# A GLA and RWKV-7 decoder layer on one core: one bit-trick step less in the inverse square root, the gate's scale folded into other factors, and pairs of half-width steps joined into one

## The chip, the core and the metric

The kernel runs on one core of one Trainium2 chip. A core has a matrix engine (TensorE, shown as PE for its matmuls and PEld for its weight loads), a vector engine (VectorE, DVE), a scalar engine (ScalarE, ACT), a general engine (GpSimd, POOL) and a queue that issues transfers (SyncE, SP). Each engine works through its own list of instructions in order, and semaphores make one engine wait for another. The metric is the device time of one launch in microseconds (us); lower is better.

## The reference, cut to what matters

One decoder layer over 4096 positions and 1024 channels. One input projection feeds two groups of heads: four heads of gated linear attention (GLA) and eight heads of RWKV-7. Both are gated with SiLU, joined and projected out. The parts that the change touches are these lines of RWKV-7 (per head of width 64):

```python
kk = kk / jnp.maximum(jnp.linalg.norm(kk, axis=-1, keepdims=True), 1e-12)
y = _rwkv7_scan(r_h, decay, k_h, v_h, kk, a)     # S_t = S_{t-1}(diag(w) - kk^T(a kk)) + v^T k
y = ((y - mu) * lax.rsqrt(var + RWKV_GN_EPS)).reshape(B, T, RWKV_W)
y = y * rwkv_ln_w + rwkv_ln_b
bonus = jnp.sum(r_h * k_h * rwkv_r_k, axis=-1, keepdims=True) * v_h
rwkv_out = (y + bonus) * jax.nn.silu(rg)
```

The norms of the layer (input, GLA heads, RWKV heads, the key norm `kk`, output) each need an inverse square root.

## The kernel before, in words

The sequence is cut into 8 blocks of 512 positions. In each block, the RWKV side has 4 units (pairs of heads; 128 partitions hold both heads, 64 each), so 32 units in all, and the GLA side has 2 pairs of heads. A unit's 512 positions are 8 chunks of 64. Projections are done in fp16 with the weights and the inputs split in a high and a low part (three products each, 24 matmuls of 128x512 per projection); the recurrences are in fp32.

The work of one RWKV unit, in the functions that the change touches:

- `newton` (lines 620 to 634) makes an inverse square root on DVE from sums of squares that a matmul with ones has left in PSUM: nine steps on tiles of 128x128. The first writes the value `nv`; the second shifts its bits right by one into `nt`; the third makes the first guess `ny` from `nt`; two rounds of three steps each refine it. It is called with three sets of tiles: `nya` (the key norm, 32 calls), `nyc` (the heads' norm after the recurrence, 32) and `nyg` (GLA heads, block input and block output, 32).
- `rwkv_ab` (780) makes a unit's operands: `rk`, `rn`, `E`, `kf`, `r`, `v`, `bk`, `De`, `Do`, the matrix `Nb`, the gate `rgs` and the bonus. The bonus is a row sum (`brow`, copied by ACT out of PSUM), written to memory, read back broadcast as `bv` (two transfers on SP's queue), and multiplied by `v`.
- `rwkv_i` (911) completes a 64x64 triangular inverse for each of 8 chunks and 2 heads from its two 32x32 diagonal blocks: DVE transposes one block (`Ta`), 16 matmuls make a product in rows 32 to 63 and 96 to 127 of a bank (`bank<-Ta,Nb`), DVE copies it (`Vs`, two copies of 32x256), 16 more matmuls (`bank<-Nb,Vs`) and two copies by ACT put the result in `Nb`.
- `rwkv_c` (935) runs the recurrence, 8 chunks in a chain. In each chunk PE makes `ch<-sv,De` and `ch<-sv,Do` for the two heads, ACT copies `us`, PE makes `ch<-us,Nb`, ACT makes two copies into `sv`, PE makes `ch<-sv,bk`, and DVE writes the next state `sv` with one SCALAR_TENSOR_TENSOR per head, which adds `psd`, the old state times the decay `PC`. ACT makes `psd` beside the chain, one step of 64x64 per head.
- `rwkv_d` (977) takes the recurrence's output `cy` and its square `crs`, takes the norm by `newton`, and then has four steps of 128x512 on DVE: `cy` times the norm; times `ln_w`, plus `bv`; plus `ln_b`, times the scale of the gate (`hinv`, half the inverse of the gate weights' scale); times the gate `rgs`, into `mgr`.

The order of the work isn't written by hand. The program first runs as eight generators (`stream_x` and its neighbours, 1306 to 1380) that take turns by priority. Each operation is recorded as a step with an estimated duration from `cost` (312). Then a list scheduler (`forward` and `backward`, 234 and 284) lays all steps out once forward, once back from the end and once forward again, and the instructions are issued, engine by engine, in the order of those estimated starts. So a changed cost or a removed step can move every later instruction on every engine, while what each instruction waits for stays bound to its data. A line of a helper that calls each recorded operation (368) is what the profile shows for nearly all instructions; they are told apart by their tiles.

PSUM has six shared banks for projections and small products, one bank for the recurrence's products (`ch`) and one for its output (`y`).

Of the kernel before, what the change touches and what calls it, by code (L numbers as in the profile page):

```python
# [20 lines left out]
P = 128  # L21
# [29 lines left out]
W_R, W_RK, W_RV, W_RG = 1, 5, 9, 13  # L51
# [9 lines left out]
PK_LW = 33  # L61
PK_LB = 37
# [18 lines left out]
def hymba_kernel(ctx, tc, xT, wt, wg, wo, wua, gup, pk, ck, out):  # L81
# [5 lines left out]
    one = ctx.enter_context(tc.tile_pool(name="one", bufs=1))  # L87
# [7 lines left out]

    TABLES = ("pkt", "scl", "invs", "hinv", "mu_s", "omu_s", "carry", "wosc", "woinv", "gnh")
    now = [0.0]
    streams = []  # L100
    ready, used, busy = {}, {}, {}
# [210 lines left out]
    def cost(eng, op, ins, n, o):  # L312

        big = [a for a in ins if math.prod(a.shape[1:]) > 1 or n == 1]
        few = len(ins) - len(big)
        psum = any(a.space == PSUM for a in ins)
        if eng == "V":
            fast = len(big) == 1 and not psum and op in ("tensor_scalar", "tensor_copy", "tensor_scalar_mul", "tensor_scalar_max")
            if op == "tensor_tensor_scan":
                return 0.068 + n / 480  # L320
            runs = 0.09 if n == 64 or len(o.shape) > 2 and o.shape[-1] == 64 and n == 512 else 0.0
            return 0.068 + 0.06 * (few > 0) + n / (1920 if fast else 960) + runs
        if eng == "G":
            return 0.225 + 0.07 * few + n * (2.13 if len(big) > 1 else 0.95) / 960
        return (0.1 if n == 64 and o.shape[0] == 64 else 0.0) + (0.052 if psum else 0.094) + n / 1200 + 0.09 * (few > 0)
# [143 lines left out]
    carry = sb(one, [P, 13], F32, "carry")  # L469
    V.memset(carry, 0.0)  # L470
    gnh = sb(one, [P, 4], F32, "gnh")


    Sst = [sb(one, [P, 64], F32, f"Sst{p}") for p in range(4)]
# [80 lines left out]
    def split_w(n, i):  # L555
        raw, hl = raws[n % 4], hls[n % 2]
        junk = hl.rearrange("p a k t -> p (a k t)").bitcast(F32).rearrange("p (k t) -> p k t", k=KT)
        iv = invs[:, i:i + 1]
        yield from absmax_scale(raw, scl[:, i:i + 1], iv, "W", junk)
        w = [hl[:, 0], hl[:, 1]]  # L560
        if n < ND:

            st = "r" if i < W_Q else "g"
            k = made[st]
            made[st] += 1
            if got[st] < k + (st == "g"):
                yield lambda: got[st] >= k + (st == "g")
            w = first[i] = pair(st)
        split(raw, scl[:, i:i + 1], *w)
        V.tensor_scalar(iv, iv, nwx[:, 9:10], 0.125 if W_Q <= i < W_K else 1.0, ALU.mult, ALU.mult)  # L570
        if W_R <= i < W_RG or i == W_WA:
            j = i - 1 if i else 12
            V.tensor_tensor(mu_s[:, j:j + 1], pkt[:, j:j + 1], iv, ALU.mult)
            V.tensor_tensor(omu_s[:, j:j + 1], omu[:, j:j + 1], iv, ALU.mult)
        elif i >= W_GG or W_RG <= i < W_Q:
            V.tensor_scalar_mul(hinv[:, i:i + 1], iv, 0.5)
            if i >= W_GG:
                h = i - W_GG
                V.tensor_tensor(gnh[:, h:h + 1], hinv[:, i:i + 1], pkt[:, PK_GN:PK_GN + 1], ALU.mult)
        if n < ND:  # L580
            for a in range(2):
                D.dma_start(wdr[i][a], w[a])
            split_done.add(i)
            done["W"] += 1
        else:
            store_w(i, hl)
# [33 lines left out]
    def newton(src, mul, add, mx, st):  # L620

        v = sb(rt, [P, P], F32, "nv" + NEWTON[st])
        y = sb(rt, [P, P], F32, "ny" + st)
        t = sb(rt, [P, P], F32, "nt" + NEWTON[st])
        if mx is not None:
            V.tensor_scalar_max(v, src, mx)
        else:
            V.tensor_scalar(v, src, mul, add, ALU.mult, ALU.add)
        V.tensor_scalar(t.bitcast(I32), v.bitcast(I32), 1, None, ALU.logical_shift_right)
        V.tensor_scalar(y.bitcast(I32), t.bitcast(I32), -1.0, float(0x5F1FFFF9), ALU.mult, ALU.add)  # L630
        for a, c in ((-0.703952253, 1.681913948), (-0.5, 1.5000003)):
            V.tensor_tensor(t, y, y, ALU.mult)
            V.scalar_tensor_tensor(t, t, a, v, ALU.mult, ALU.mult)
            V.scalar_tensor_tensor(y, t, c, y, ALU.add, ALU.mult)
        return y
# [144 lines left out]
    def rwkv_ab(u, p, b, xs, LR):  # L780
# [102 lines left out]
        pst = yield from need("r")  # L883
        stat_mm(pst, bones, r)
        brow = sb(rt, [P, P], F32, "brow", 1)
        S.copy(brow, pst[:, 0:P])
        bv = tA("bv", 2)
        bcast(brow, 2, bv, "b")
        V.tensor_tensor(bv, bv, v, ALU.mult)
# [21 lines left out]
    def rwkv_i(nb):  # L911

        Ta = sb(rt, [P, NC, 32], F32, "Ta", 1)
        Vs = sb(rt, [P, NC, 32], F32, "Vs", 1)
        yield after(nb)
        for q0 in (0, 64):
            V.transpose(Ta[q0:q0 + 32], nb[q0:q0 + 32, :, q0:q0 + 32])
        yield after(Ta)
        pl = (yield from need("i")).rearrange("p (a c t) -> p a c t", a=2, c=NC)
        for c in range(NC):  # L920
            for q0 in (0, 64):
                T.matmul(pl[q0 + 32:q0 + 64, 0, c, :], lhsT=nb[q0:q0 + 32, c, q0 + 32:q0 + 64], rhs=Ta[q0:q0 + 32, c, :],
                         start=True, stop=True)
        for q0 in (0, 64):
            V.tensor_copy(Vs[q0 + 32:q0 + 64], pl[q0 + 32:q0 + 64, 0])
        yield after(Vs)
        for c in range(NC):
            for q0 in (0, 64):
                T.matmul(pl[q0:q0 + 32, 1, c, :], lhsT=Vs[q0 + 32:q0 + 64, c, :], rhs=nb[q0 + 32:q0 + 64, c, q0 + 32:q0 + 64],
                         start=True, stop=True)  # L930
        for q0 in (0, 64):
            S.copy(nb[q0:q0 + 32, :, q0 + 32:q0 + 64], pl[q0:q0 + 32, 1])
        rel("i")

    def rwkv_c(p, b, mgt, st_):
        de, do, nb, sv, bkt, PC, bv, tg = st_
        yield after(nb, bkt, sv, ("y", 1))

        py = pbank("y").rearrange("p (c t) -> p c t", c=NC)
        st = Sst[p]  # L940
        S.copy(sv[0:64, 0, 0, :], st[0:64])
        V.tensor_copy(sv[64:128, 0, 1, :], st[64:128])
        dd = ((lo, de, 0), (hi, do, 1))
        for c in range(NC):
            pc = pbank("ch").rearrange("p (a t) -> p a t", a=8)
            for q_, d_, e in dd:
                T.matmul(pc[q_, 0, :], lhsT=d_[:, c, 0:64], rhs=sv[:, c, e, :], start=True, stop=True)
            us = sb(rt, [P, 64], F32, "us", 2)
            S.copy(us, pc[:, 0, :])
            for q_, d_, e in dd:  # L950
                T.matmul(py[q_, c, :], lhsT=sv[:, c, e, :], rhs=d_[:, c, 64:128], start=c == 0, stop=False)
            psd = sb(rt, [P, 64], F32, "psd", 2)
            for q_, d_, e in dd:
                S.activation(psd[q_], sv[q_, c, e, :], AF.Copy, scale=PC[q_, c])
            yield after(us) + XL
            T.matmul(pc[:, 1, :], lhsT=nb[:, c, 0:P], rhs=us, start=True, stop=True)
            S.copy(sv[lo, c, 0, :], pc[lo, 1, :])
            S.copy(sv[hi, c, 1, :], pc[hi, 1, :])
            yield after(sv) + XL
            T.matmul(pc[:, 2:4, :], lhsT=bkt[:, c, :], rhs=sv[:, c], start=True, stop=True)  # L960
            for q_, d_, e in dd:
                dst = sv[q_, c + 1, e, :] if c < NC - 1 else st[q_]
                V.scalar_tensor_tensor(dst, pc[q_, 2 + e, :], PC[q_, c], psd[q_], ALU.mult, ALU.add)
            if c < NC - 1:
                yield after(sv, ("ch", 1)) + XL
        for c in range(NC):
            for q_, d_, e in dd:
                T.matmul(py[q_, c, :], lhsT=sv[q_, c, e, :], rhs=nb[q_, c, P:192], start=False, stop=c == NC - 1)
        yield lambda: done["C"] == done["CC"]
        y = sb(rt, [P, TB], F32, "cy")  # L970
        rs = sb(rt, [P, TB], F32, "crs")
        S.copy(y, py.rearrange("p c t -> p (c t)"))
        S.activation(rs, y, AF.Square)
        done["CC"] += 1
        spawn(rwkv_d(p, b, mgt, y, rs, bv, tg), 2.5)

    def rwkv_d(p, b, mgt, y, rs, bv, tg):
# [11 lines left out]
            bcast(st, 2, rs, "c")  # L989
        V.tensor_tensor(y, y, rs, ALU.mult)  # L990
        rel("d")
        V.scalar_tensor_tensor(y, y, pkt[:, PK_LW + p:PK_LW + p + 1], bv, ALU.mult, ALU.add)
        i = W_RG + p
        V.tensor_scalar(y, y, pkt[:, PK_LB + p:PK_LB + p + 1], hinv[:, i:i + 1], ALU.add, ALU.mult)
        yield lambda: len(mfree["r"]) > 0
        mgt[4 + p] = mfree["r"].pop(0)
        V.tensor_tensor(mgt[4 + p], y, tg, ALU.mult)
        absmax(mgt, 4 + p, y)
        done["C"] += 1

# [453 lines left out]
```

## Time and profile before

| What | Before |
|---|---|
| median of 3 runs | 2419.3 us (2418.5 to 2422.08) |
| time of the profiled execution | 2425.58 us |
| its span, from the first instruction to the last | 2423.8 us |
| granted TensorE clock, mean | 0.982 |
| PE busy | 2301.9 us, 20710 matmul records |
| DVE busy | 1691.6 us |
| ACT busy | 1219.0 us |
| POOL busy | 851.4 us |

The profile comes from one execution, 1.8 us of which lie outside its span. A PE that is busy isn't always at its peak, since the ends of matmuls are modelled. In the groups of instructions, a row reads: line, engine, operation, tile written <- tiles read, shape, count, then busy time in us and the mean of one in ns, then the engine's idle time just before them and what ended it. An fp32 matmul has two records, one for each of its passes.

### The profile page before, as it was taken

The numbers are of one execution on the slowest core, as the hardware profiler recorded it, in microseconds if no ns is written. First come the engines' busy times: TensorE is split into PE (matmuls) and PEld (weight loads), VectorE is DVE, ScalarE is ACT, GpSimd is POOL, SyncE is SP. The second block draws the span as 40 slices with busy tenths as digits, with TensorE's granted clock in tenths as the row PEclk, the third lists the DMA queues.
The fourth block names the chain that finished last, engine by engine and source line by source line (L and its number), as shares of the span: only waits on it lengthen the run. The fifth ranks groups of instructions, "written<-read, shape, count | busy, mean of one in ns | idle before, by whom it ended". The sixth has DMA issues, their size and how long they took to land.

```text
span 2423.8 us, 54428 instructions
## 1 busy us (share of the span) xinstructions
PE 2301.9 (95%) x20710; PEld 1344.5 (55%) x20710; DVE 1691.6 (70%) x3866; ACT 1219.0 (50%) x3123; POOL 851.4 (35%) x2217
## 2 busy tenths in 40 slices
PE   7899999999999999999999999999999998999986
PEld 3555565455555656545564555645565564654643
DVE  7877877568675776676675687666867577666755
ACT  7576565455454555444644545455445455534342
POOL 4442234434323533315334243343334353331300
PEclk9898999999999999999999999999999999999987
DMA  6675545355334543455424553345533454344431
GB/s 196 205 229 184 160 145 172 110 170 151 95 102 129 169 126 97 112 145 168 112 80 122 171 151 103 98 124 162 151 94 98 130 182 116 104 109 116 137 91 58
DMA packets 275387, 325.54 MB, mean 134 GB/s; under 512 B 131652, under 2 KB 132788, under 8 KB 275124
## 3 DMA queue, kind: packets, MB, share of 16 engines
q1 hardware_dynamic: 275124, 322.06, 46.0%
q8 instruction: 162, 2.65, 0.5%
q14 instruction: 101, 0.83, 0.1%
HBM read 276.90 MB, written 45.05 MB: 133 GB/s over the span
## 4 chain that ended last, share of the span: by engine, by line
PE 63%; DVE 22%; DMA 6%; ACT 5%; issue 2%; SPq 1%; POOL 1%; DVEq 0%; ACTq 0%; POOLq 0%
PE bank L368 56%; PE ch L368 6%; DVE nta L368 2%; PE y L368 2%; DVE bk L368 2%; DVE Nb L368 2%; DVE De L368 1%; DVE Do L368 1%; DVE mgg L368 1%; DVE mgr L368 1%; DMA bv<-bcdb 1%; DVE gbc L368 1%; SPq L368 1%; DVE cy L368 1%; DVE sv L368 1%
## 5 line engine op out<-in xcount | busy, mean ns | idle before, releaser
L368 PE MATMUL bank<-x,wr 128*128 128x512 f16 x3264 | 811.3, 382 | 13.2 <-DVE De L368 5.7
L368 POOL TENSOR_TENSOR tm<-Tc,f 128x60 f32<-128x60 f32 (+24 forms) x961 | 338.5, 352 | 661.7 <-DMA f<-nd 405.5
L368 PEld LDWEIGHTS <-wr 128*128 128x128 f16 x3264 | 309.1, 100 | 319.2 <-issue 32.4
L368 PE MATMUL bank<-x,wg 128*128 128x512 f16 x1536 | 388.8, 380 | 5.4 <-DMA wg<-wdr 4.4
L368 POOL TENSOR_TENSOR Tc<-Tc,tm 128x60 f32<-128x60 f32 (+24 forms) x961 | 342.3, 356 | 73.2
L368 PE MATMUL bank<-x,wo 128*128 128x512 f16 x1488 | 364.0, 385 | 0.7 <-DVE nva L368 0.5
L368 DVE SCALAR_TENSOR_TENSOR sv<-ch,PC,psd 64x64 f32<-64x64 f32 x448 | 126.2, 282 | 214.5 <-PE ch L368 205.9
L368 POOL TENSOR_TENSOR xacc<-xacc,xr 128x512 f32<-128x512 f32 x98 | 131.8, 1345 | 374.0 <-ACT xr L368 211.5
L368 ACT ACTIVATE psd<-sv,PC 64x64 f32<-64x64 f32 x512 | 171.6, 342 | 122.3 <-DVE sv L368 115.4
L368 PEld LDWEIGHTS <-wg 128*128 128x128 f16 x1536 | 143.8, 99 | 152.1 <-issue 9.6
L368 PEld LDWEIGHTS <-wo 128*128 128x128 f16 x1488 | 143.0, 101 | 143.4 <-issue 9.3
L368 PEld LDWEIGHTS <-x 128*128 128x128 f16 x3120 | 189.8, 99 | 33.1 <-issue 13.4
L368 PE MATMUL bank<-wg,x 128*128 128x128 f16 x3072 | 206.2, 220 | 1.7 <-DMA wg<-wdr 1.7
L368 ACT COPY sv<-ch 64x64 f32<-64x64 f32 x512 | 104.6, 204 | 100.2 <-PE ch L368 93.1
L368 ACT ACTIVATE sa<-bank,mu_s 128x512 f32<-128x512 f32 x104 | 71.5, 687 | 137.0 <-PE bank L368 135.7
L368 POOL MEMSET Tc<- 32x8 f32 (+1 forms) x160 | 23.6, 148 | 318.2 <-DMA td<-Tc 303.5
L368 PEld LDWEIGHTS ch<-us,Nb 128*128 128x128 f32 x512 | 87.2, 191 | 57.2 <-ACT us L368 42.7
L368 ACT COPY us<-ch 128x64 f32<-128x64 f32 x256 | 53.3, 208 | 125.0 <-PE ch L368 122.4
L368 PEld LDWEIGHTS ch<-sv,bk 128*128 128x128 f32 x512 | 89.4, 191 | 48.1 <-ACT sv L368 32.7
L368 PE MATMUL ch<-sv,bk 128*128 128x128 f32 x512 | 106.8, 291 | 5.6 <-ACT sv L368 5.6
L368 PE MATMUL ch<-us,Nb 128*128 128x64 f32 x512 | 95.6, 269 | 11.5 <-ACT us L368 9.1
L368 PEld LDWEIGHTS ch<-sv,De 128*64 128x64 f32 x512 | 49.3, 135 | 98.9 <-issue 42.6
(327 smaller groups left out, 4115.4 us busy)
## 6 DMA issues: line engine op xcount, KB each, us to landing
wr<-wdr SPq DMA_DIRECT2D x256, 256.0 KB
wg<-wdr SPq DMA_DIRECT2D x184, 256.0 KB
xr<-in_xT_dram SPq DMA_DIRECT2D x176, 256.0 KB
wo<-wdr SPq DMA_DIRECT2D x128, 256.0 KB
f<-nd SPq DMA_DIRECT2D x128, 128.0 KB
x<-in_wt_dram SPq DMA_DIRECT2D x29, 512.0 KB
wdr<-wo SPq DMA_DIRECT2D x25, 512.0 KB
out_dram<-mgg SPq DMA_DIRECT2D x33, 256.0 KB
```

The source lines that it names most:

```text
L368: put(t0, self.name, d, lag, cols, tiles, tab, outs, ins, lambda: f(*a, **kw))
```

## The change

Five edits of the computation, and one of the planner's costs:

1. `newton` no longer shifts. The first guess comes straight from the bits of `nv`, multiplied by -0.5 instead of -1 after a shift.
2. The gate's scale goes into three other factors. `ln_w` and `ln_b` are multiplied by it once per weight tile at setup (`lnh`, eight products of 128x1), and `brow` is multiplied by it in the step that copies it out of PSUM. The step of `rwkv_d` that added `ln_b` and multiplied by the scale goes away; the last step adds the scaled `ln_b` and multiplies by the gate in one SCALAR_TENSOR_TENSOR.
3. `psd` is made by one ACT step of 128x128 over both heads' states; each head still reads its own half of it.
4. In `rwkv_i`, the first product covers all 64 rows of each head instead of its lower 32: the stationary operand has 64 columns instead of 32. One copy of 128x256 takes the place of two of 32x256.
5. In `rwkv_c`, the square `crs` is read from PSUM, ahead of the copy `cy`, instead of from `cy` behind it.
6. `cost` gets terms for a predicated copy, for transposes and PSUM reads of 32x256, and for a two-scalar step, so the planner lays everything out anew.

```diff
@@ def cost
             runs = 0.09 if n == 64 or len(o.shape) > 2 and o.shape[-1] == 64 and n == 512 else 0.0
+            if op == "copy_predicated":
+                runs = 0.09
+            elif n == 256 and o.shape[0] != 128:
+                runs += 0.04 if op == "transpose" else 0.09
+            elif op == "tensor_scalar" and few > 1:
+                runs = 0.06
@@ def split_w
+            else:
+                for j in range(i - W_RG, 8, 4):
+                    V.tensor_tensor(lnh[:, j:j + 1], hinv[:, i:i + 1], pkt[:, PK_LW + j:PK_LW + j + 1], ALU.mult)
@@ def newton
-        V.tensor_scalar(t.bitcast(I32), v.bitcast(I32), 1, None, ALU.logical_shift_right)
-        V.tensor_scalar(y.bitcast(I32), t.bitcast(I32), -1.0, float(0x5F1FFFF9), ALU.mult, ALU.add)
+        V.tensor_scalar(y.bitcast(I32), v.bitcast(I32), -0.5, float(0x5F1FFFF9), ALU.mult, ALU.add)
@@ def rwkv_ab
-        S.copy(brow, pst[:, 0:P])
+        S.activation(brow, pst[:, 0:P], AF.Copy, scale=hinv[:, i:i + 1])
@@ def rwkv_i
-                T.matmul(pl[q0 + 32:q0 + 64, 0, c, :], lhsT=nb[q0:q0 + 32, c, q0 + 32:q0 + 64], rhs=Ta[q0:q0 + 32, c, :],
+                T.matmul(pl[q0:q0 + 64, 0, c, :], lhsT=nb[q0:q0 + 32, c, q0:q0 + 64], rhs=Ta[q0:q0 + 32, c, :],
                          start=True, stop=True)
-        for q0 in (0, 64):
-            V.tensor_copy(Vs[q0 + 32:q0 + 64], pl[q0 + 32:q0 + 64, 0])
+        V.tensor_copy(Vs, pl[:, 0])
@@ def rwkv_c
-            psd = sb(rt, [P, 64], F32, "psd", 2)
-            for q_, d_, e in dd:
-                S.activation(psd[q_], sv[q_, c, e, :], AF.Copy, scale=PC[q_, c])
+            psd = sb(rt, [P, 2, 64], F32, "psd", 2)
+            S.activation(psd, sv[:, c], AF.Copy, scale=PC[:, c])
...
-                V.scalar_tensor_tensor(dst, pc[q_, 2 + e, :], PC[q_, c], psd[q_], ALU.mult, ALU.add)
+                V.scalar_tensor_tensor(dst, pc[q_, 2 + e, :], PC[q_, c], psd[q_, e], ALU.mult, ALU.add)
...
+        S.activation(rs, py.rearrange("p c t -> p (c t)"), AF.Square)
         S.copy(y, py.rearrange("p c t -> p (c t)"))
-        S.activation(rs, y, AF.Square)
@@ def rwkv_d
-        V.scalar_tensor_tensor(y, y, pkt[:, PK_LW + p:PK_LW + p + 1], bv, ALU.mult, ALU.add)
-        i = W_RG + p
-        V.tensor_scalar(y, y, pkt[:, PK_LB + p:PK_LB + p + 1], hinv[:, i:i + 1], ALU.add, ALU.mult)
+        V.scalar_tensor_tensor(y, y, lnh[:, p:p + 1], bv, ALU.mult, ALU.add)
...
-        V.tensor_tensor(mgt[4 + p], y, tg, ALU.mult)
+        V.scalar_tensor_tensor(mgt[4 + p], y, lnh[:, 4 + p:5 + p], tg, ALU.add, ALU.mult)
```

The number of instructions changes on DVE (3868 to 3716) and ACT (3008 to 2752) alone. PE has the same matmuls, 512 of them in the new shape, and the order on all engines is new. Three places show the kinds of movement.

First PE, at the inverse of the last unit, before. `Ta` and `Vs` are the inverse's tiles, `ch` and `y` those of the recurrence of the unit ahead of it:

```order
L368 MATMUL ch_266<-sv_255,De_0_128 64x64
L368 MATMUL ch_266<-sv_255,Do_0_130 64x64
L368 MATMUL y_265<-De_0_128,sv_255 64x64
L368 MATMUL y_265<-Do_0_130,sv_255 64x64
L368 MATMUL bank_0_185<-Ta_257,Nb_0_133 32x32 x16
L368 MATMUL ch_266<-us_267,Nb_0_132 128x64
L368 MATMUL bank_0_185<-Nb_0_133,Vs_258 32x32
L368 MATMUL ch_266<-sv_255,bk_237 128x128
L368 MATMUL bank_0_185<-Nb_0_133,Vs_258 32x32 x15
```

And the same place after the change:

```order
L374 MATMUL ch_267<-sv_256,De_0_129 64x64
L374 MATMUL ch_267<-sv_256,Do_0_131 64x64
L374 MATMUL y_266<-De_0_129,sv_256 64x64
L374 MATMUL y_266<-Do_0_131,sv_256 64x64
L374 MATMUL bank_0_181<-Ta_258,Nb_0_134 64x32 x16
L374 MATMUL ch_267<-us_269,Nb_0_133 128x64
L374 MATMUL bank_0_181<-Nb_0_134,Vs_259 32x32 x16
L374 MATMUL ch_267<-sv_256,bk_238 128x128
```

The sixteen first products are now 64x32; all sixteen second products stand together ahead of the recurrence's `ch<-sv,bk`, which stood behind the first of them.

Second DVE, at the end of the last unit's norm, before (`nta` and `nyc` are `newton`'s tiles, `amo` the maximum that the output projection's scale needs):

```order
L368 SCALAR_TENSOR_TENSOR nta_207<-nta_207,nva_205 128x128
L368 SCALAR_TENSOR_TENSOR Sst_0_125<-ch_266,PC_232,psd_270 64x64
L368 SCALAR_TENSOR_TENSOR nyc_273<-nta_207,nyc_273 128x128
L368 TENSOR_TENSOR cy_199<-cy_199,bank_0_181 128x512
L368 SCALAR_TENSOR_TENSOR cy_199<-cy_199,pkt_95,bv_252 128x512
L368 TENSOR_SCALAR cy_199<-cy_199,pkt_95,hinv_119 128x512
L368 TENSOR_TENSOR mgr_0_91<-cy_199,rgs_249 128x512
L368 TENSOR_REDUCE amo_282<-mxs_0_187 128x1
```

After:

```order
L374 SCALAR_TENSOR_TENSOR Sst_0_126<-ch_267,PC_233,psd_271 64x64
L374 SCALAR_TENSOR_TENSOR nta_208<-nta_208,nva_206 128x128
L374 SCALAR_TENSOR_TENSOR nyc_274<-nta_208,nyc_274 128x128
L374 TENSOR_TENSOR cy_200<-cy_200,bank_0_181 128x512
L374 SCALAR_TENSOR_TENSOR cy_200<-cy_200,lnh_122,bv_253 128x512
L374 SCALAR_TENSOR_TENSOR mgr_0_91<-cy_200,lnh_122,rgs_250 128x512
L374 TENSOR_REDUCE amo_283<-mxs_0_188 128x1
```

Three steps of 128x512 are left of four; the last state write `Sst` has moved one place up.

Third ACT, in the recurrence of the last unit, before:

```order
L368 COPY sv_256<-ch_266 64x64 x2
L368 ACTIVATE psd_270<-sv_256,PC_232 64x64 x2
L368 COPY us_268<-ch_266 128x64
L368 COPY sv_256<-ch_266 64x64 x2
L368 ACTIVATE psd_269<-sv_256,PC_232 64x64 x2
```

After:

```order
L374 COPY sv_257<-ch_267 64x64 x2
L374 ACTIVATE psd_271<-sv_257,PC_233 128x128
L374 COPY us_269<-ch_267 128x64
L374 COPY sv_257<-ch_267 64x64 x2
L374 ACTIVATE psd_270<-sv_257,PC_233 128x128
```

One step of 128x128 stands where two of 64x64 stood, in the same place ahead of `us`.

More of the change, by code (lines that the diff above doesn't have):

```diff
@@ L93, in hymba_kernel @@
     psp = ctx.enter_context(tc.tile_pool(name="psp", bufs=1, space=PSUM))
-    TABLES = ("pkt", "scl", "invs", "hinv", "mu_s", "omu_s", "carry", "wosc", "woinv", "gnh")
+    TABLES = ("pkt", "scl", "invs", "hinv", "mu_s", "omu_s", "carry", "wosc", "woinv", "gnh", "lnh")
     now = [0.0]
@@ L471, in hymba_kernel @@
     gnh = sb(one, [P, 4], F32, "gnh")
+    lnh = sb(one, [P, 8], F32, "lnh")
     Sst = [sb(one, [P, 64], F32, f"Sst{p}") for p in range(4)]
```

## The prediction

> **What bounds the kernel now.** I read the page's busy shares first, then the granted clock and busy time by stage, then the chain of work that ended last, then what PE waited for.
>
> The page's first part:
>
> ```profile
> PE 2301.9 (95%) x20710; PEld 1344.5 (55%) x20710; DVE 1691.6 (70%) x3866; ACT 1219.0 (50%) x3123; POOL 851.4 (35%) x2217
> ```
>
> Three stretches (setup, the steady middle, the end); columns are length, busy time of PE, PEld, DVE, ACT and POOL, then clock, DMA share and GB/s:
>
> ```profile
> 0.00:240.00 240.00, 206.20 (x1662) 121.93 (x1662) 188.26 (x525) 157.16 (x317) 91.42 (x212) 0.94 0.66 204
> 240.00:2280.00 2040.00, 1982.63 (x18117) 1158.61 (x18114) 1419.98 (x3110) 1014.70 (x2673) 757.61 (x1995) 1.00 0.46 130
> 2280.00:2423.80 143.80, 113.03 (x935) 63.97 (x934) 83.32 (x233) 47.15 (x133) 2.33 (x12) 0.85 0.28 78
> ```
>
> PE is busy in 1982.6 of 2040 us of the middle, at full clock. All that faster DVE and ACT work can give there is a part of the 57 us in which PE stands; 34 us stand in setup and 31 at the end, so 122 in all. The chain, by engine and by line:
>
> ```profile
> PE 63%; DVE 22%; DMA 6%; ACT 5%; issue 2%; SPq 1%; POOL 1%; DVEq 0%; ACTq 0%; POOLq 0%
> PE bank L368 56%; PE ch L368 6%; DVE nta L368 2%; PE y L368 2%; DVE bk L368 2%; DVE Nb L368 2%; DVE De L368 1%; DVE Do L368 1%; DVE mgg L368 1%; DVE mgr L368 1%; DMA bv<-bcdb 1%; DVE gbc L368 1%; SPq L368 1%; DVE cy L368 1%; DVE sv L368 1%
> ```
>
> What PE itself waited for (total us, times, longest):
>
> ```profile
> PE bank L368 <- DVE bk L368: 15.5, 10, 6.0
> PE ch L368 <- DVE sv L368: 9.7, 17, 2.9
> PE ch L368 <- ACT us L368: 9.1, 19, 1.8
> PE bank L368 <- DVE De L368: 8.9, 7, 3.4
> PE bank L368 <- DVE amo L368: 6.8, 4, 3.9
> ...
> PE bank L368 <- DVE Vs L368: 5.6, 10, 1.2
> ...
> PE ch L368 <- ACT sv L368: 5.6, 10, 0.8
> ```
>
> So DVE is late oftener than ACT, in many short waits, and no single one is worth 1%. About 0.2% (4.8 us) is what a measurement of this kernel tells from no change.
>
> **The change part by part.**
>
> *The shift.* The rows of `newton`'s tile `nt` on DVE:
>
> ```profile
> L368 DVE SCALAR_TENSOR_TENSOR nta<-nta,nva 128x128 f32<-128x128 f32 x192 | 59.4, 309 | 4.0
> L368 DVE TENSOR_SCALAR nta<-nva 128x128 int32<-128x128 int32 x96 | 25.8, 269 | 1.9
> L368 DVE TENSOR_TENSOR nta<-nya 128x128 f32<-128x128 f32 x64 | 22.8, 356 | 1.3
> L368 DVE TENSOR_TENSOR nta<-nyg 128x128 f32<-128x128 f32 x64 | 19.8, 309 | 1.4
> L368 DVE TENSOR_TENSOR nta<-nyc 128x128 f32<-128x128 f32 x64 | 18.8, 294 | 1.0
> ```
>
> 96 steps of 269 ns go, 25.8 us. These rows sum to 146.6 us, of which the shift is 17.6%; the chain gives `nta` 2% of 2423.8, 48 us, so 8.5 us of shifts lie on the chain. The rest is hidden by PE's other matmuls. With a shift gone, a chain that ran beside it is late next, usually PE's own queue, so I take 5 of the 8.5: **-5** (ends -8.5 and 0).
>
> *The gate's scale.* The rows of `rwkv_d` that go or change:
>
> ```profile
> L368 DVE SCALAR_TENSOR_TENSOR cy<-cy,pkt,bv 128x512 f32<-128x512 f32 x32 | 24.5, 765 | 0.7
> L368 DVE TENSOR_TENSOR cy<-cy,crs 128x512 f32<-128x512 f32 x31 | 21.4, 689 | 35.2 <-DMA crs<-bcdc 35.1
> L368 DVE TENSOR_SCALAR cy<-cy,pkt,hinv 128x512 f32<-128x512 f32 x32 | 17.4, 543 | 0.6
> L368 DVE TENSOR_TENSOR gnh<-hinv,pkt 128x1 f32<-128x1 f32 x4 | 0.8, 196 | 0.1
> ```
>
> 32 steps of 543 ns go, 17.4 us, or 27% of the three rows' 63.3. `cy` has 1% of the chain, 24 us, so 6.6 us of the step lie on it. But only each block's last unit has the output projection waiting for it, so I take **-2** (ends -6.6 and 0). The last step becomes a SCALAR_TENSOR_TENSOR: by the rows above 765 instead of 689 ns, +2.4 us on DVE in all. Eight products at setup add 8 x 0.196 = 1.6 us there. `brow`, 268 ns now, gets a scale:
>
> ```profile
> L368 ACT COPY brow<-bank 128x128 f32<-128x128 f32 x32 | 8.6, 268 | 33.6 <-PE bank L368 33.5
> L368 ACT ACTIVATE gbc<-gbc,nm 128x128 f32<-128x128 f32 x64 | 25.6, 399 | 1.3
> L368 ACT ACTIVATE psd<-sv,PC 64x64 f32<-64x64 f32 x512 | 171.6, 342 | 122.3 <-DVE sv L368 115.4
> ```
>
> By the second row, of the same size, it may take 399 ns: 32 x 0.13 = 4.2 us more, ahead of `brow`'s transfers. Together **+0.5**; PE's queue covers the rest (end +4).
>
> *`psd`.* By the last two rows, 256 steps of about 399 ns (102 us) take the place of 512 of 342 (171.6): 69 us off ACT. But look at a chunk:
>
> ```profile
> 1518.34 0.60 DVE L368 SCALAR_TENSOR_TENSOR sv<-ch,PC,psd 64x64 f32<-64x64 f32 x2 [2.53 <-PE ch L368]
> ...
> 1519.01 0.71 ACT L368 ACTIVATE psd<-sv,PC 64x64 f32<-64x64 f32 x2
> ...
> 1520.34 0.21 ACT L368 COPY us<-ch 128x64 f32<-128x64 f32 x1 [0.35 <-PE ch L368]
> ```
>
> The pair ends at 1519.72; the next copy on ACT's path starts at 1520.34 and waited for PE. 0.3 us saved there is saved from waiting. It counts where ACT was late: 29 times PE waited for `us` or `sv`, 14.7 us in all, and 29 x 0.29 = 8.4 us could go. I take **-2.5** (ends -8.4 and 0).
>
> *One copy `Vs`.*
>
> ```profile
> L368 DVE COPY Vs<-bank 32x256 f32<-32x256 f32 x64 | 27.1, 423 | 8.4 <-PE bank L368 7.3
> L368 PEld LDWEIGHTS bank<-Ta,Nb 32*32 32x32 f32 x1024 | 19.9, 109 | 15.2 <-issue 4.2 <-DVE Ta L368 2.5 <-DVE De L368 2.0
> L368 PEld LDWEIGHTS y<-Nb,sv 64*64 64x64 f32 x1024 | 32.9, 134 | 9.8 <-issue 8.3
> L368 PE MATMUL bank<-Ta,Nb 32*32 32x32 f32 x1024 | 24.2, 194 | 2.7 <-DVE De L368 1.4 <-DVE Ta L368 1.3
> L368 PE MATMUL y<-Nb,sv 64*64 64x64 f32 x1024 | 37.5, 221 | 0.0
> ```
>
> A copy of 423 ns goes in each unit, 13.5 us of DVE, and PE waited for it 10 times, 5.6 us in all: 10 x 0.42 = 4.2 us. **-4** (ends -5.6 and 0).
>
> *The price of it, on PE.* The first products keep their count and their 32 moving columns, but each loads 64 stationary columns instead of 32. No row has that pair of widths. The nearest, `y<-Nb,sv`, has 64 and 64, with as many records: 134 ns per load against 109, 37.5 us of PE against 24.2. So the ends are 0, if the shorter stream still sets the pace, and **+13.3**, if the loads do. Two neighbours differ in pace here:
>
> ```profile
> 1520.79 0.33 PE L368 MATMUL ch<-us,Nb 128*128 128x64 f32 x2
> ...
> 1521.82 0.39 PE L368 MATMUL ch<-sv,bk 128*128 128x128 f32 x2
> ```
>
> Both load 128 columns; with 64 moving columns the pair of passes is 0.06 us shorter than with 128, so a load doesn't wholly set the pace of a pair. I take two thirds, **+9**. Nothing hides it: it stands in PE's queue, behind it everything on PE, and the copy `Vs` starts later by as much. The Trainium skill speaks against the change here: "TensorE: Matmul & The Clock Gate", section "LDWEIGHTS (loading the stationary operand)", puts a load's time at its columns over 1.2 per ns, so 32 more columns are 27 ns; the rows' 134 less 109 agree. By that rule alone, 32 units of 16 passes in pairs would cost an estimated 13.7 us, and the sum would be 4.7 us higher.
>
> *The end.* Nothing covers the last unit's norm:
>
> ```profile
> 2384.63 0.58 ACT L368 COPY cy<-y 128x512 f32<-128x512 f32 x1 [1.54 <-PE y L368]
> ...
> 2394.72 0.55 DVE L368 TENSOR_SCALAR cy<-cy,pkt,hinv 128x512 f32<-128x512 f32 x1
> ...
> 2410.05 0.23 DVE L368 TENSOR_SCALAR nta<-nva 128x128 int32<-128x128 int32 x1
> ```
>
> The third row's shift and the like one before it (0.46), the second row, and part of the first (the square no longer waits for it) go: **-1.5**.
>
> *The new order.* The planner lays everything out anew. PE changes from one kind of matmul to another 3778 times instead of 3795, which is nothing. Where waits fall changes everywhere; I take 0, with 6 us either way.
>
> Sum: -5 - 2 + 0.5 - 2.5 - 4 + 9 - 1.5 = **-5.5 us**. The profiled execution took 2425.6, so 2420.1 in its terms; it lies 6.3 us over the median of the runs shown, 2419.3, so the forecast on the median is **2413.8**.
>
> **The rivals.**
>
> *The wider loads set the pace (slower).* In the first products of the inverse, loads of 64 columns go at the pace of `y<-Nb,sv`: the full +13.3. For it: PE is busy in 97% of the middle, so its time counts one for one. If then only the waits pay that are direct (`Vs` -4, end -1.5), the sum is +7.8, so **2427**. It decides the sign when the group of 32 passes, 24.2 / 32 = 0.76 us per unit now, grows by more than (4.8 + 5.5) / 32 = 0.32 us in that case. Against: the shorter stream may still hide a part of each load, as in the pair of passes above. The section of the Trainium skill named above ("TensorE: Matmul & The Clock Gate", LDWEIGHTS) would have this rival come true.
>
> *Nothing to gain (no change).* The freed time lies in waiting, as at `psd`'s chunk above; direct waits (-5.5) pay for loads of half the bound (+6.7). Then the sum is about +1, so **2420**. The chain's 63% on PE speaks for it.
>
> *The loads are hidden and the chain's shares come off whole (much faster).* -8.5 - 6.6 - 5.6 - 1.5 = -22: **2397**. For it: `nta` and `cy` are named in the chain. Against: the chain is one of several that are nearly as late.
>
> **How the numbers follow.** Chances: the forecast 0.42, the slower rival 0.20, no change 0.18, much faster 0.20. With 6 us for the order either way, the forecast lies beyond 4.8 us faster in 0.24 of its 0.42 and within 0.2% in 0.18; "no change" spreads as 0.03, 0.11 and 0.04. So faster is 0.24 + 0.20 + 0.03 = 0.47, same 0.18 + 0.11 = 0.29, slower 0.20 + 0.04 = 0.24. The range goes from just below the much faster case to the slower one with a part of the order's 6 us: 2396 to 2430.
>
> **What would show it.** Right: the group `bank<-Ta,Nb` 32*64 at about 33 us of PE, DVE at about 1640 us, ACT at about 1150, PE's waits for `Vs` near 1 and those for `bk` and `De` below 24; PE's busy time up and its idle time down by more. Wrong: that group at 37 or more with idle time unchanged (slower rival), or idle time lower by 20 with the group at 24 (much faster). Waits on PE that weren't in the list before, above 5 us, would lay the difference to the new order.

## The result and the profile after

The changed kernel takes **2388.5 us** (median of 4 runs, 2382.6 to 2389.7), the kernel before 2419.6 in the runs beside it: a ratio of 0.9865, 95% interval [0.9847, 0.9883]. That is about 31 us faster, more than five times the forecast 5.5 us and below the range's lower end of 2396. Two executions at a much lower granted clock (0.85 and 0.20; 2592 and 10849 us) are left out of all medians and intervals here.

The page of the changed kernel, first the busy times by engine, then the chain that ended last by engine:

```profile
PE 2294.4 (96%) x20710; PEld 1352.6 (57%) x20710; DVE 1650.4 (69%) x3714; ACT 1142.1 (48%) x2867; POOL 865.2 (36%) x2217
...
PE 66%; DVE 18%; DMA 7%; ACT 5%; issue 2%; POOL 1%; SPq 1%; DVEq 0%; ACTq 0%; POOLq 0%
```

DVE lost 41 us, where some 52 were forecast, and ACT 77, where some 69 were. (In the run `old_order_new_work` below, which keeps the old order, DVE is busy for 1642.0 us, near the forecast 1640.) The two spans are 35.9 us apart, 5 more than the medians, since the profiled execution of before lies 6 us over its median. PE did not go up by the price of its wider loads: it went down by 7.5 us, and its idle time fell from 121.9 to 93.5 us (2387.9 - 2294.4). DVE's part of the chain fell from 22% to 18%. By stage, with the columns of the prediction's table:

```profile
0.00:240.00 240.00, 203.91 (x1691) 123.62 (x1691) 183.51 (x523) 149.43 (x292) 87.41 (x183) 0.95 0.65 203
240.00:2280.00 2040.00, 2009.06 (x18361) 1183.28 (x18360) 1407.06 (x3040) 959.58 (x2480) 777.80 (x2034) 1.00 0.46 131
2280.00:2387.90 107.90, 81.44 (x662) 45.70 (x660) 59.88 (x153) 33.09 (x96) 0.00 (x0) 0.84 0.29 84
```

In the same 2040 us of the middle PE is now busy in 2009 instead of 1983: it stands for 31 us instead of 57, and what is left over for the last stretch is 36 us shorter. Counted in matmul records, PE is 29 ahead of the kernel before at 240 us and 273 ahead at 2280 us. So most of the gain was made in the steady middle. The mean granted clock rose too, from 0.982 to 0.987. It isn't what made the gain: two of the runs below, `new_order_old_work` and `narrow_one_copy`, both have 0.985 in their profiles, and lie 48 us apart. The groups that the change made, one row each of PE, its loads, ACT and DVE:

```profile
L374 PE MATMUL bank<-Ta,Nb 32*64 32x32 f32 x1024 | 37.0, 219 | 0.2 <-DVE Ta L374 0.2
...
L374 PEld LDWEIGHTS bank<-Ta,Nb 32*64 32x64 f32 x1024 | 33.0, 133 | 11.1 <-issue 4.3 <-DVE Ta L374 2.0 <-DVE nyc L374 1.2
...
L374 ACT ACTIVATE psd<-sv,PC 128x128 f32<-128x128 f32 x256 | 99.3, 397 | 164.8 <-DVE sv L374 163.5
...
L374 DVE COPY Vs<-bank 128x256 f32<-128x256 f32 x32 | 13.4, 419 | 20.3 <-PE bank L374 20.2
```

The first products went from 24.2 to 37.0 us of PE: the wider loads do set the pace, as the slower rival had it. And what PE waited for (total us, times, longest):

```profile
PE bank L374 <- DVE bk L374: 10.1, 10, 3.8
PE bank L374 <- ACT wo L374: 8.6, 7, 3.4
PE ch L374 <- DVE sv L374: 8.6, 12, 1.7
PE ch L374 <- ACT us L374: 6.1, 13, 0.9
PE bank L374 <- ACT x L374: 5.3, 4, 1.9
PE bank L374 <- DVE amo L374: 4.7, 3, 3.4
PE ch L374 <- ACT sv L374: 4.6, 11, 0.9
```

`bk` went from 15.5 to 10.1, `us` and `sv` from ACT from 14.7 together to 10.7. `De` went from 8.9 to 1.3 and `Vs` from 5.6 to 0.2; the wait for ACT's `wo`, the output projection's weights, grew from 2.1 to 8.6.

So 12.8 us of dearer PE work were paid, and over 40 us came from elsewhere. The runs had to tell from where.

### The profile page after: what moved, and what is told of

Its sections match the earlier page's. It is cut to its first block, busy times and chain, and to the rows that moved or that the text cites. A ratio compares the mean times of both kernels' runs of the same rounds, so it can differ in the third digit from the quotient of the medians.

```text
span 2387.9 us, 54083 instructions
## 1 busy us (share of the span) xinstructions
PE 2294.4 (96%) x20710; PEld 1352.6 (57%) x20710; DVE 1650.4 (69%) x3714; ACT 1142.1 (48%) x2867; POOL 865.2 (36%) x2217
## 4 chain that ended last, share of the span: by engine, by line
PE 66%; DVE 18%; DMA 7%; ACT 5%; issue 2%; POOL 1%; SPq 1%; DVEq 0%; ACTq 0%; POOLq 0%
PE bank L374 58%; PE ch L374 6%; PE y L374 2%; DVE nta L374 2%; DVE bk L374 1%; DVE Nb L374 1%; DVE Do L374 1%; SPq L374 1%; DVE De L374 1%; DVE mgr L374 1%; DVE mgg L374 1%; DVE E L374 1%; DMA bv<-bcdb 1%; DVE sv L374 1%; DMA xr<-in_xT_dram 1%
## 5 line engine op out<-in xcount | busy, mean ns | idle before, releaser
L374 POOL TENSOR_TENSOR Tc<-Tc,tm 128x60 f32<-128x60 f32 (+24 forms) x961 | 354.3, 369 | 73.6
L374 PE MATMUL bank<-wg,x 128*128 128x128 f16 x3072 | 200.2, 221 | 1.5 <-DMA wg<-wdr 1.5
L374 ACT ACTIVATE psd<-sv,PC 128x128 f32<-128x128 f32 x256 | 99.3, 397 | 164.8 <-DVE sv L374 163.5
```

The source lines that it names most:

```text
L374: put(t0, self.name, d, lag, cols, tiles, tab, outs, ins, lambda: f(*a, **kw))
```

## The experiments

All compare with the kernel before in runs beside them, whose median lay between 2419.1 and 2421.3 us. An interval is about 0.15% (3.6 us) either way, so a difference of two kernels carries some 5 us. A price in us is a difference of medians; where the ratios, which compare with the kernel before in the same runs, give another figure, it stands beside it. To hold an order fixed, a kernel plans each step as the kernel whose order it keeps, and only what the planned step then issues is replaced (`emit`):

```diff
-                put(t0, self.name, d, lag, cols, tiles, tab, outs, ins, lambda: f(*a, **kw))
+                put(t0, self.name, d, lag, cols, tiles, tab, outs, ins, emit.pop() if emit else lambda: f(*a, **kw))
```

**The order or the work.** Four kernels: the new order with all the old work, the old order with all the new work, and the planner's new costs alone and left out.

```diff
 new_order_old_work: the changed kernel; each edited step is planned as it is there and issues the old steps
 old_order_new_work: the kernel before; each edited step is planned as it is there and issues the new one
 costs_only: the kernel before, and in cost():
+            if op == "copy_predicated":
+                runs = 0.09
+            elif n == 256 and o.shape[0] != 128:
+                runs += 0.04 if op == "transpose" else 0.09
+            elif op == "tensor_scalar" and few > 1:
+                runs = 0.06
 edits_old_costs: the changed kernel without these six lines
```

> The changed kernel's order on PE, POOL and SP to the instruction, with the old work put back at its places: the shift, the step of the norm with the gate's scale, two steps for the decay, 32-column loads with two copies, the square behind the copy. If the freed work makes the gain (theory W), this loses most of it: 2410 to 2425 us, DVE busy near 1692, ACT near 1219, the group Ta,Nb back at 24 us. If the new order makes it (theory O), it stays within 8 us of the changed kernel, 2380 to 2397 us; the 13 us of PE that the narrower loads give back could even make it 2375.

> The order of before on PE, POOL and SP to the instruction, with all five edits of the computation. Theory W: 2385 to 2400 us. Theory O: the freed work pays only for the wider loads, 2412 to 2425 us, which is also what the prediction's sum says without its term for the order (2414).

> The kernel before with the planner's new costs alone, all work as before. Theory O, if it is the better costs that make the order good: 2385 to 2400 us. Theory W: within 6 us of before, 2414 to 2426 us. If any new order may be lucky or unlucky (theory L): anywhere within about 10 us of before.

> All five edits of the computation with the planner's old costs, laid out anew. Theory W: 2385 to 2400 us. Theory O with the costs as its cause: 2410 to 2422 us. If the planner gains from both, some 2400 us.

| median, us (ratio) | old work | new work |
|---|---|---|
| old order | 2419.6 | 2399.8 (0.9909 [0.9886, 0.9931]) |
| new order | 2425.9 (1.0019 [1.0008, 1.0030]) | 2388.5 (0.9865) |

The planner's costs alone gave 2411.4 (0.9961 [0.9945, 0.9977]), 10 us under the 2421.3 beside it; but all edits with the old costs gave 2389.2 (0.9868 [0.9848, 0.9887]), as with the new ones. So the gain isn't the costs', and it isn't the order's as such, which is slower with the old work (by 4.5 us against the 2421.3 beside it). It is the freed work: 22 us in the old order, 37 in the new one. The other 10 us or so come with laying the lighter work out anew; for this pair, the order and the work are not independent. The new order with the old work, its busy times, its chain by engine and PE's waits:

```profile
PE 2296.6 (95%) x20710; PEld 1336.5 (55%) x20710; DVE 1707.6 (71%) x3874; ACT 1223.8 (51%) x3123; POOL 857.5 (35%) x2217
...
PE 54%; DVE 28%; ACT 9%; DMA 5%; issue 3%; SPq 1%; POOL 0%; DVEq 0%; POOLq 0%; ACTq 0%
```

```profile
PE ch L375 <- ACT us L375: 15.2, 34, 1.3
PE ch L375 <- DVE sv L375: 12.2, 22, 1.6
PE bank L375 <- DVE bk L375: 10.2, 8, 4.0
```

With PE's matmuls in the same order (the inverse's first products 32 columns wide), PE's part of the chain is 54% in place of 66%, and the recurrence's waits for ACT's `us` are 15.2 us in place of 6.1.

**Each edit put back alone, in the new order.** With `emit`, one planned step of the changed kernel issues the old ones:

```diff
 psd_back
+            def two(psd=psd, c=c):
+                for q_, d_, e in dd:
+                    s_.activation(psd[q_, e], sv[q_, c, e, :], AF.Copy, scale=PC[q_, c])
 shift_back
+            v_.tensor_scalar(y.bitcast(I32), v.bitcast(I32), 1, None, ALU.logical_shift_right)
+            v_.tensor_scalar(y.bitcast(I32), y.bitcast(I32), -1.0, float(0x5F1FFFF9), ALU.mult, ALU.add)
 scale_back
+            v_.scalar_tensor_tensor(y, y, pkt[:, PK_LW + p:PK_LW + p + 1], bv, ALU.mult, ALU.add)
+            v_.tensor_scalar(y, y, pkt[:, PK_LB + p:PK_LB + p + 1], hinv[:, i:i + 1], ALU.add, ALU.mult)
+        emit.append(lambda: v_.tensor_tensor(mgt[4 + p], y, tg, ALU.mult))
+        emit.append(lambda pst=pst, brow=brow: s_.copy(brow, pst[:, 0:P]))
 inv_back
+                emit.append(lambda c=c, q0=q0: t_e.matmul(pl[q0 + 32:q0 + 64, 0, c, :], lhsT=nb[q0:q0 + 32, c, q0 + 32:q0 + 64], ...
+                v_.tensor_copy(Vs[q0 + 32:q0 + 64], pl[q0 + 32:q0 + 64, 0])
```

> The changed kernel, every engine's order as it is there, but each of the 256 scaled state copies psd is made again as two 64x64 steps (2 x 342 ns on ACT in place of 397), so ACT has some 72 us more. The prediction put this step of the change at 2.5 us, 8.4 at most, since most of it is time in which ACT waits for PE anyway: then 2391 to 2397. Theory A (the recurrence: ACT's freed time is what pays, since the next chunk's copies queue behind psd): most of the 37 us that all old work costs in this order come from here, 2410 to 2420. Theory V (VectorE's freed 41 us are what pays, as the chain of waits had VectorE at 22% and ACT at 5%): as the prediction, 2389 to 2397.

> The changed kernel in its own order, but the inverse square root has its shift back: 96 steps of 0.27 us on VectorE, 25.8 us. The prediction put it at 5 us, 8.5 at most: 2393.5 (to 2397). Theory V (VectorE's freed time pays nearly whole): 2404 to 2412. Theory A (ACT's psd pays): 2389 to 2393.

> The changed kernel in its own order, but with the gate's scale as a step of its own again in the group norm (32 steps of 0.54 us on VectorE, 17.4 us) and brow copied without a scale. The prediction put it at 2 - 0.5 = 1.5 us (6.6 at most): 2390 (to 2395). Theory V: 2396 to 2404. Theory A: 2388 to 2391.

> The changed kernel in its own order, but the first products of the inverse load 32 columns again and Vs is copied in two steps of 0.42 us: takes 12.8 us off PE (37.0 back to 24.2) and puts 13.5 us on VectorE, 0.42 us of it in each unit between two groups of PE's. The prediction had -9 and +4, so this edit undone would be 5 us faster: 2383.5. If PE's 12.8 us count whole and the copies only by the 4 us of waits: 2380. Theory V (VectorE's time counts nearly whole): 2386 to 2390. If the loads were hidden after all, it is slower: 2392 to 2400.

Measured: `psd_back` 2396.8 (0.9902 [0.9889, 0.9915]), so 8.2 us; `shift_back` 2400.3 (0.9919 [0.9907, 0.9931]), 11.8; `scale_back` 2395.9 (0.9899 [0.9883, 0.9916]), 7.4; `inv_back` 2379.1 (0.9831 [0.9819, 0.9843]), which is 9.5 us *faster* than the changed kernel. By the ratios the four are 9.0, 13.1, 8.2 and -8.2. Neither theory V (DVE alone pays) nor A (ACT alone) holds: all three pay. PE's waits show where. With `psd` in two steps:

```profile
PE ch L375 <- ACT us L375: 13.2, 29, 1.3
...
PE ch L375 <- ACT sv L375: 4.3, 10, 0.9
```

Against 6.1 and 4.6 that is 6.8 of the 8.2 us, in the recurrence's waits for ACT. With the shift:

```profile
PE bank L375 <- DVE bk L375: 12.9, 12, 4.0
PE ch L375 <- DVE sv L375: 10.8, 19, 1.6
...
PE ch L375 <- ACT sv L375: 6.0, 12, 1.6
```

Here 6.4 us of the 11.8 stand in three waits, none of which is for the inverse square root itself.

**The loads and the copy apart; three edits together; other orders.**

```diff
 narrow_one_copy: the changed kernel, one planned matmul issued with 32 columns, the one copy kept
+                emit.append(lambda c=c, q0=q0: t_e.matmul(pl[q0 + 32:q0 + 64, 0, c, :], lhsT=nb[q0:q0 + 32, c, q0 + 32:q0 + 64],
+                                                          rhs=Ta[q0:q0 + 32, c, :], start=True, stop=True))
 three_back: shift_back, scale_back and psd_back together (and cy's square taken from the copy)
 after_nudge, before_nudge: the changed kernel, and the kernel before, with
-            return 0.068 + 0.06 * (few > 0) + n / (1920 if fast else 960) + runs
+            return 0.07 + 0.06 * (few > 0) + n / (1920 if fast else 960) + runs
```

> The changed kernel in its own order, with the first products of the inverse loading 32 columns again, as before the change, but Vs still copied in one step of 0.42 us (the 32 rows of each 64 that this product doesn't write are copied along and not used). So it differs from the changed kernel in the loads alone, and from the run with the whole inverse put back in the second copy alone. If the 12.8 us that the wider loads add on PE count one for one: 2375.5. If the loads were partly covered, by a half: 2382. If the second copy costs its 13.5 us of VectorE at the 0.44 us per us that the shift and the gate's scale showed (11.8 of 25.8 and 7.4 of 17.4): 2379.1 - 5.9 = 2373.

> The changed kernel in its own order with the shift, the gate's own step and the two psd steps back together (and the square of cy taken from its copy again), the inverse as changed. Put back one by one these cost 11.8, 7.4 and 8.2 us. If they add: 2388.5 + 27.4 = 2416. If freed time on the two engines is worth more the less there is of it (the cover is used up): all old work together was 2425.9 and the old inverse alone saves 9.5, so 2435. If they overlap (each hides behind the other): 2400 to 2410.

> The changed kernel, with the planner's fixed cost of a VectorE step at 0.070 us in place of 0.068: the same work in another order of about as good a plan. If an order's place among like ones is worth 6 us either way, as the prediction had it: 2382.5 to 2394.5. If this plan is a lucky one: 2395 to 2410. If it is an average one: 2384 to 2393.

> The kernel before, with the planner's fixed cost of a VectorE step at 0.070 us in place of 0.068: the same work in another order. With 6 us either way: 2413.4 to 2425.4. If the plan of before was an unlucky one (old work in the order of the new costs took 2411.4): 2405 to 2415.

`narrow_one_copy` took 2377.7 (0.9830 [0.9816, 0.9843]): 10.8 us less than the changed kernel (8.5 by the ratios) from the loads alone, most of the 13.9 us that they cost on PE in this order (37.0 against the 23.1 below), and 1.3 us less than `inv_back`, which is what the second copy is worth (within the uncertainty, nothing). Its busy times and its first products:

```profile
PE 2282.2 (96%) x20710; PEld 1339.7 (56%) x20710; DVE 1652.4 (70%) x3714; ACT 1143.2 (48%) x2867; POOL 864.1 (36%) x2217
```

```profile
L933 PE MATMUL bank<-Ta,Nb 32*32 32x32 f32 x1024 | 23.1, 192 | 0.3 <-DVE Ta L375 0.2
```

This kernel's PE has just the matmuls of the kernel before, and is busy for 19.7 us less (2301.9 before) and idle for 28.9 us less. Some 8 to 9 us of the 19.7 can be the granted clock, 0.982 of the one span and 0.985 of the other (43.6 and some 35 us of full clock not granted). But `new_order_old_work` has the same matmuls, in the same order, at the same 0.985, and is busy for 14.4 us more (2296.6). So the busy time of PE in the page holds more than the work of its matmuls, and time in which PE stands is no bound on the gain by itself, though no run here gained more than the 57 us. The Trainium skill says in "Perfetto Trace Analysis", section "Identifying the Most-Contended Engine", that matmul busy time is no good measure of how near the engine is to its peak, since matmuls are pipelined; the 14.4 us agree.

`three_back` took 2429.2 (1.0035 [1.0021, 1.0048]): 40.7 us over the changed kernel, where 11.8 + 7.4 + 8.2 = 27.4 were to be expected if the edits added. Its busy times and chain by engine, then PE's waits:

```profile
PE 2306.9 (95%) x20710; PEld 1353.4 (56%) x20710; DVE 1690.2 (70%) x3842; ACT 1224.1 (50%) x3123; POOL 860.5 (35%) x2217
...
PE 56%; DVE 24%; DMA 8%; ACT 8%; issue 3%; SPq 1%; POOL 0%; DVEq 0%; POOLq 0%; ACTq 0%
```

```profile
PE ch L375 <- ACT us L375: 16.9, 36, 1.6
PE ch L375 <- DVE sv L375: 13.4, 21, 1.6
PE bank L375 <- DVE bk L375: 13.0, 11, 4.0
...
PE bank L375 <- ACT crs L992: 5.8, 10, 1.6
```

Of the 42.2 us between the two profiled spans (2430.1 and 2387.9), 12.5 are in PE's busy time (2306.9 - 2294.4) and the rest is idle. The 13.3 us over the sum are less firm than the 40.7. The scatter of the changed kernel's own median enters them twice, so they are known to some 10 us only. And `three_back` puts back the square of `cy` too, which no run has alone: PE's waits for its result `crs` are 5.8 us here and 2.1 in the changed kernel. The old inverse put back into this company (which gives `new_order_old_work`) saves only 3.3 us more, not 9.5. That would fit a PE whose own work counts less where it waits more, but the difference is about what such a comparison carries.

`after_nudge` took 2382.6 (0.9848 [0.9835, 0.9862]) and `before_nudge` 2413.4 (0.9975 [0.9964, 0.9985]): each some 6 us below its kernel (4 by the ratio for the changed one, within the uncertainty). With `costs_only` and `edits_old_costs` there are three plans for either work: 2411 to 2421 us with the old, 2383 to 2389 with the new, 29 us apart by the mean of their ratios. So the gain is no luck of one order, though the plan of the kernel before is the slowest of its three.

**Why the shift pays, and where the extra comes from.** A step can cost by its own result coming later, or by what is queued behind it on its engine, or by load alone. Spare steps of the shift's form, on the mask that only DVE reads and by 0 bits, tell these apart; two pairs of edits look for the extra 13 us of the three.

```diff
+            v_.tensor_scalar(smask.bitcast(I32), smask.bitcast(I32), 0, None, ALU.logical_shift_right)
 spare_behind_newton: one behind the last step of 95 inverse square roots
 spare_ahead_of_waits: two ahead of 48 DVE steps that waited over 0.65 us (16 mgr, 15 mgg, 14 rgs, 3 bv)
 shift_scale_back, shift_psd_back: two of the edits above put back together
 spare_behind_dependent: one behind each of the 96 inverse square roots, reading its result
+                    v_.tensor_scalar(t.bitcast(I32), y.bitcast(I32), 1, None, ALU.logical_shift_right)
 narrow_nudge: narrow_one_copy planned with 0.07 in place of 0.068
```

> The changed kernel in its own order, with 95 spare steps added on VectorE of the removed shift's form and size (0.27 us each, 25.6 us, on a tile that nothing else writes, by a shift of 0 bits so that nothing changes), each behind the last step of an inverse square root, so that its result is as early as in the changed kernel and only what is queued behind on VectorE is later. The shift put back ahead cost 11.8 us. If that came from the inverse square root's own chain (its result, the broadcast and the norm behind it): 2389 to 2392 here. If it came from VectorE's queue (whatever stands behind): 2398 to 2402.

> The changed kernel in its own order, with 96 spare steps of the same form added on VectorE (25.8 us), in 48 pairs of 0.54 us, each pair ahead of a step that waited for PE, ScalarE or a DMA by over 0.65 us in every run of this order. If a step costs by what is queued behind it without a wait between: 2388 to 2391. If the load of the engine (or of the memory that it shares) is what costs, wherever it stands: 2397 to 2402.

> The changed kernel in its own order with the shift and the gate's own step both back, 43 us of VectorE. One by one 11.8 and 7.4 us. If they add: 2407.7. If the extra 13 us of the three together comes from VectorE's two edits: 2415 to 2421.

> The changed kernel in its own order with the shift and the two psd steps both back. One by one 11.8 and 8.2 us. If they add: 2408.5. If the extra 13 us of the three together comes from VectorE and ScalarE being late in turn in the recurrence (each step of it needs both): 2415 to 2422.

> The changed kernel in its own order with 96 spare shifts on VectorE, each reading the finished result of an inverse square root (so it can't overlap the step ahead of it, as the removed shift couldn't) and writing a tile that nothing reads. VectorE's busy time should rise by some 24 us, as with the shift put back (1674.5). If the shift cost by its own result coming later, this costs next to nothing: 2387 to 2392. If it cost by what is queued behind it: 2397 to 2402.

> The two findings that made the changed kernel faster, together: the first products of the inverse with 32-column loads and one copy of Vs (10.8 us less), and the plan made with 0.070 in place of 0.068 us for a VectorE step (5.9 us less). If they add: 2371.8. If the better plan hangs on the wider products' lengths, it falls to the narrow kernel's own 2377.7 or above.

The busy times, of the kernel with spares behind, and of that with spares ahead of waits:

```profile
PE 2293.1 (96%) x20710; PEld 1350.0 (57%) x20710; DVE 1663.1 (70%) x3809; ACT 1142.7 (48%) x2867; POOL 863.4 (36%) x2217
```

```profile
PE 2293.1 (96%) x20710; PEld 1350.6 (57%) x20710; DVE 1674.4 (70%) x3810; ACT 1142.0 (48%) x2867; POOL 865.5 (36%) x2217
```

24 us more on DVE ahead of its waits cost nothing: 2387.1 (0.9858 [0.9845, 0.9871]). So load alone is not what costs. The spares behind cost 1.0 us (2389.5, 0.9872 [0.9857, 0.9886]), but they raised DVE's busy time by only 12.7 us, for 95 steps of 0.22 us in the median: steps that depend on no neighbour overlap with it. Those that wait for the result ahead of them raised it by 20.2:

```profile
PE 2294.1 (96%) x20710; PEld 1349.5 (57%) x20710; DVE 1670.6 (70%) x3810; ACT 1144.1 (48%) x2867; POOL 867.8 (36%) x2217
```

and the kernel took 2392.7 (0.9884 [0.9868, 0.9901]), 4.2 us more, not told from nothing by these runs, while the shift, with 24.1 us, cost 11.8, an interval that lies above this one. So by the medians some 7.6 of the shift's 11.8 us are that its own result comes later; the intervals show that this part isn't nothing, not that it is the larger. What the shift does to the queue behind is between nothing and some 8 us.

`shift_scale_back` took 2414.8 (0.9968 [0.9955, 0.9980]), 7.1 us over the sum of the two; `shift_psd_back` 2413.7 (0.9975 [0.9964, 0.9985]), 5.2 over. Both are over it by no more than the uncertainty (3.6 and 4.6 us by the ratios), and neither has the whole 13; whether the extra is real, and where it comes from, stays open. `narrow_nudge` took 2376.6 (0.9813 [0.9799, 0.9828]): the fastest of all, but not apart from `narrow_one_copy`. The two gains don't add.

## Why the prediction was wrong, step by step

| step of the sum, us | taken | its end | measured |
|---|---|---|---|
| shift | -5 | -8.5 | -11.8 |
| gate's scale, with brow | -1.5 | -6.6 | -7.4 |
| psd | -2.5 | -8.4 | -8.2 |
| one copy Vs | -4 | -5.6 | -1.3 |
| wider loads | +9 | +13.3 | +10.8 |
| the end | -1.5 | | -0.8 (in the rows above) |
| new order | 0 | 6 either way | +4.5 with the old work, some -10 with the new |

**The step that failed is the discount.** The ends, the edit's share of its tile's time times the tile's share of the chain, or a direct wait's count times what each saves, were within 3.3 us (shift), 0.8 (scale) and 0.2 (`psd`) of what these three proved to be worth, each known to some 5 us. The prediction then took a part of each: "a chain that ran beside it is late next" (shift), "only each block's last unit has the output projection waiting for it" (scale), "saved from waiting" (`psd`). The runs show no such chain that takes the gain away: put back alone, the three cost 27.4 us where 9 were taken, and together, with the square, 40.7. For `psd`, 6.8 of its 8.2 us are found again in PE's waits. In company freed time was worth at least the sum, not less. With every gain at its end and the loads at theirs, the prediction's own sum would have been -8.5 - 6.6 - 8.4 - 5.6 - 1.5 + 13.3 = -17.3; the edits put back one by one add up to -17.9. Both come near the -22 of the old order, but that tests neither, since no edit was put back alone there.

**The bound beside it was not one.** "All that faster DVE and ACT work can give there is a part of the 57 us in which PE stands" took PE's busy time for work. With the same matmuls in the same order, `narrow_one_copy` has 14.4 us less of it than `new_order_old_work`.

**The order was taken as independent of the work.** As a scatter, 6 us was somewhat small: the nudges moved by 4 to 6 us, and `costs_only` by 10. But the old order cost the new work some 10 us and the new order cost the old work 4.5. Each fits the work that it was planned for, by 15 us in all. One pair of orders shows this; that the plan used the freed time is a likely reading, and how far it holds for others was not tried.

**The wider loads.** They cost 12.8 us of PE (24.2 to 37.0, which the sign named for the slower rival) and 10.8 of time; two thirds of the bound were too little, but by 1.8 us only. The rule of the Trainium skill weighed there ("TensorE: Matmul & The Clock Gate", "LDWEIGHTS (loading the stationary operand)"), with 13.7 us, was nearer to the group's 12.8 (13.9 with the order held) than the +9. The slower rival's mechanism came true and its sum did not: it let only direct waits pay. The "much faster" rival had the chain's shares near and the loads wrong, and its 2397 was the nearest of the four; that is luck in part, since it left out both the loads (10.8) and `psd` (8.2), which nearly cancel.

**The copy.** Ten waits for `Vs` of 5.6 us were taken for 4 us of gain. The waits went (0.2 us now), but the second copy is worth 1.3 us. In the new order the two copies, put back in `inv_back`, make PE wait for 1.7 us only, so most of the 5.6 belonged to the old order.

**The end.** From the last norm's `nva` to its `mgr`, before and after:

```profile
2386.67 0.28 DVE L368 TENSOR_SCALAR nva<-bank 128x128 f32<-128x128 f32 x1
...
2395.30 0.69 DVE L368 TENSOR_TENSOR mgr<-cy,rgs 128x512 f32<-128x512 f32 x1
```

```profile
2354.26 0.28 DVE L374 TENSOR_SCALAR nva<-bank 128x128 f32<-128x128 f32 x1
...
2361.53 0.75 DVE L374 SCALAR_TENSOR_TENSOR mgr<-cy,lnh,rgs 128x512 f32<-128x512 f32 x1
```

9.3 us have become 8.0, but not only by the edits. The shift (0.26 from its start to the next) and the gate's step (0.58) are gone and the last step is 0.06 longer, 0.8 in all; besides, three of the output's steps stand between them instead of four. The square that no longer waits gained nothing there: from the first of ACT's two steps to `nva` it is 2.04 us in both.

## What to carry to other kernels

Take an edit on a chain's path at the full share that the chain gives it, and discount it only for a second chain that can be named: here that held for three edits, and not for the copy, whose waits went with the order. Several such edits together need not be worth less than their sum, and a plan made anew for the lighter work can add to that. An engine's busy time is no floor where its work is pipelined: compare two runs with the same instructions before using its idle time as a bound. Look at each part of a merged edit apart: here the merge that saves a copy costs 10.8 us by its loads on the engine that bounds the kernel, and without it the same change gives 2377.7 instead of 2388.5.

## What the runs showed of the hardware

- In fp32 passes of 32 moving columns, a load of 64 stationary columns instead of 32 makes a pass 36.1 ns instead of 23.6 (37.0 and 24.2 us over 1024), the load itself 133 instead of 109 ns. The passes start in pairs, 6 to 7 ns apart, and two times 12.5 ns is about the 24 ns that a load has grown by: so short a stream hides almost nothing of the wider load.
- On ACT a scaled copy of 128x128 takes 397 ns and one of 64x64 343, four times the elements for 54 ns: there the number of steps is most of the cost, not their size.
- On DVE, 95 independent steps with a median duration of 219 ns added 12.7 us of busy time, 0.13 us each; 96 of the same form that wait for the step ahead added 20.2, 0.21 each. So a step's duration in the profile comes near to what it takes of the engine only where it depends on its neighbour.
